# MLP up projection of a two-layer decoder trunk: high and low part of the input as one 512-column operand

## The chip, the cores and the metric

The kernel runs on one core of a Trainium2 chip. The metric is the device time of one execution in microseconds (us); lower is better. The time before is the median of three runs, 669.83 us (669.26 to 670.19). One further execution was profiled; its own time was 669.9 us.

## The reference: what is computed

The program is a decoder trunk with DEPTH = 2 layers over x of 256 tokens by 1024 features, float32. Each layer has a mixer (three kinds of attention heads that share one input and one output projection) and a gated MLP with a causal depthwise convolution of width 3; both are added to x. Cut to the MLP:

```python
def conv_glu_ffn(h, w_up, conv_w, conv_b, w_down):
    a, u = jnp.split(h @ w_up, 2, axis=-1)          # h: 256 x 1024, w_up: 1024 x 5632
    a = causal_depthwise_conv(a, conv_w) + conv_b    # width 3, per channel
    return (jax.nn.silu(a) * u) @ w_down             # w_down: 2816 x 1024

for i in range(DEPTH):
    x = x + hybrid_mixer(rmsnorm(x, norm1_g[i]), ...) @ w_out[i]
    x = x + conv_glu_ffn(rmsnorm(x, norm2_g[i]), w_up[i], conv_w[i], conv_b[i], w_down[i])
return rmsnorm(x, final_g)
```

## The kernel before

**Split operands.** Every large matrix product works on float32 numbers that are split in two: a high part, the value rounded to the fp32r format, and a low part, what the rounding left. A product is the sum of three: high by high, high by low, low by high. `weight` (L146 and behind) loads a weight tile by DMA into a staging buffer `st` (5 buffers, queue of SP), writes its high part into `hl` with a cast on ACT (L157) and its low part with a subtraction on DVE (L159). There are 8 buffers `hl`; a cast has to wait until an earlier tile's last matmul on PE has freed one. The activations are split in `transposed`: high by ACT (`ahi`, L195), low by DVE (`alo`, L196), with the tokens along the columns. Two functions hand out those tiles: `act_half` (four blocks of 128 features by 256 tokens, one tile for the high and one for the low parts) and `act_pair` (two halves, so all 1024 features).

**The MLP.** The 2816 channels are done in 11 groups f of 256 channels. `up(f)` loads four weight tiles of w_up (gate half `a` and value half `u`, each in two tiles of four feature blocks) and two tiles of w_down. For each of the two halves `au` and the two blocks of 128 channels `s` it runs over the eight blocks k of 128 features; each k takes three matmuls with 128 weight columns and 256 moving columns: high weights by `hhi` (L896), high weights by `hlo` (L897), low weights by `hhi` (L898). The sums stay in PSUM: one bank for `a` and one for `u`, each with s = 0 in the left 256 columns and s = 1 in the right. Roles u0 and u1 of two banks each take turns with f.

Behind the matmuls DVE multiplies `a` by the normalisation factors R (L900), ACT and DVE do the convolution (L906, L908), ACT a tanh (L911), DVE finishes the gate (L912), multiplies `u` by R/2 (L914) and by the gate (L915), and ACT and DVE split the product into `h_hi` (L919) and `h_lo` (L920).

`down(f)` multiplies h by the w_down rows of that group: 24 matmuls of 512 columns (L206 to L208, in `mm3`) into four banks `bn` that add up over all f. The loop runs `up(f)` and then `down(f - 1)`, so a group's elementwise work has a whole `up` to run beside. The last two groups' `down` comes at the end of the layer.

**What sets the order.** The tile framework orders each engine's instructions when the program is built and puts in the waits; at run time each engine takes its list in that order. DVE, ACT and PE each work in order, so an instruction that waits holds up all that stand behind it on its engine.

Of the kernel before, what the change touches and what calls it, by code (L numbers as in the profile page):

```python
# [12 lines left out]
F32 = mybir.dt.float32  # L13
FR = mybir.dt.float32r
BF = mybir.dt.bfloat16
AF = mybir.ActivationFunctionType
OP = mybir.AluOpType
AX = mybir.AxisListType

L = 256  # L20
# [50 lines left out]
def trunk(ctx, tc, x, norm1_g, w_in, cmp_pos, cmp_w1, cmp_w2, w_out, norm2_g, w_up, conv_w, conv_b, w_down,  # L71
          final_g, eye, consts_f, consts_b, out):
    nc = tc.nc
    V, S, G, PE = nc.vector, nc.scalar, nc.gpsimd, nc.tensor
# [3 lines left out]
    act = ctx.enter_context(tc.tile_pool(name="act", bufs=1))  # L78

    def banks(es, *layout):  # L80

        pools = {r: es.enter_context(tc.tile_pool(name="ps_" + r, bufs=n, space=bass.MemoryType.PSUM,
                                                  reuse_waits="tile")) for r, n in layout}
        return lambda r: pools[r].tile([128, 512], F32, name="b" + r, tag=r)
# [53 lines left out]
    def columns(b, dst, src):  # L138
        n = src.shape[0]
        PE.transpose(b[:, :n], src, ident[:n, :n])  # L140
        V.tensor_copy(dst, b[:, :n])


    def after(ins):
        return tc.issue_after(ins) if ins else nullcontext()
# [16 lines left out]
    def w_in_chunk(i, c0, n, then=None, behind=(None, None)):  # L162
        w = w_in[i].rearrange("(k p) c -> p k c", p=128)
        return [weight(w[:, 2 * h:2 * h + 2, c0:c0 + n], 2, n, then if h == 0 else None, behind)
                for h in range(4)]
# [15 lines left out]
    def new_ssq():  # L181
        return keep.tile([128, 2, 2], F32, name="ssq", tag="ssq", bufs=2)
# [14 lines left out]
        return l0, l1  # L197

    def act_half():
        return [act.tile([128, 4, L], FR, name=n, tag=n, bufs=3) for n in ("ahi", "alo")]  # L200

    def act_pair():
        return tuple(zip(act_half(), act_half()))
# [6 lines left out]
    for i in range(DEPTH):  # L210

        with ExitStack() as es:
            if i == 0:
                bank = banks(es, ("t", 2), ("d", 2), ("s", 2), ("o", 2))
            else:
                bank = banks(es, ("d", 2), ("s", 2), ("t", 2), ("o", 2))
# [5 lines left out]
            if i == 0:  # L222

                def idle(n):
                    b = bank("d")
                    for j in range(n):
                        PE.matmul(b[:, :256], zero[:, 0:128], zero, start=j == 0, stop=j == n - 1)

                idle(16)
                columns(bank("t"), cola[:, 0:16], rn)  # L230

                def other_half():
                    nc.scalar.dma_start(xr[:, 0, 512:D], x[0, 0:128, 512:D])
                    nc.sync.dma_start(xr[:, 1, 512:D], x[0, 128:256, 512:D])

                first = w_in_chunk(0, 0, 384, other_half)
                ssq = new_ssq()
                hhi, hlo = act_pair()
                for k0 in (0, 2, 4, 6):
                    last = transposed(bank, xr, gain1[i], hhi, hlo, k0, 2, role="tsso"[k0 // 2])  # L240
                idle(8)
                for t in range(2):
                    for n in range(2):
                        junk = pj.tile([128, 512], BF, name="junkv", tag="selb")
                        xs = xr[:, t, n * 512:(n + 1) * 512]
                        if n == 0:
                            with after(last[0].ins):
                                s0 = sumsq(ssq, t, n)
                            continue
                        with after(last[1].ins):  # L250
                            s1 = V.scalar_tensor_tensor(junk, xs, 1.0, xs, op0=OP.mult, op1=OP.mult,
                                                   accum_out=ssq[:, t, n:n + 1])
                squares = s0.ins, s1.ins
# [148 lines left out]
            def runs_of(segs):  # L402
# [5 lines left out]
                        r.append((t, [h], o, nk // 128))  # L408
                return r

            m0 = act_half()

            vv = pj.tile([128, 3, 2, 64], F32, name="vv")

# [349 lines left out]
            for _ in indexed(ob):  # L764
                fill(1)
            fill()
            m1 = act_half()
            ob = [o.rearrange("p c t q -> p c (t q)") for o in ob]
            split([z[64:128, 2:4, :] for z in m0], ob[0][64:128])
            split([z[0:64, 3, :] for z in m0], ob[0][0:64, 0])  # L770
# [77 lines left out]
            fill()  # L848
            dense.append(out_part((5, 6), (7,)))
            fill(3)  # L850
            hhi, hlo = act_pair()

            def half2(n):
                for t in range(2):
# [8 lines left out]
            R = keep.tile([128, 2, L], F32, name="R", tag="R", bufs=1)  # L863
            b = bank("t")
            for t in range(2):
                PE.matmul(b[:, t * 128:(t + 1) * 128], rstd[:, t:t + 1].to_broadcast([128, 128]), ident,
                          start=True, stop=True)
            S.copy(R[:, 0, :], b[:, :256])
            G.tensor_copy(R[:, 1, :], R[:, 0, :])
            R = R.rearrange("p a c -> p (a c)")  # L870


        with ExitStack() as es:
            order = ("n0", "n1", "u0", "u1") if i == 0 else ("n0", "u0", "n1", "u1")
            bank = banks(es, *((r, 2) for r in order))
            mp = es.enter_context(tc.tile_pool(name="mp", bufs=2, reuse_waits="tile"))
            dn = {}
            NF = DFF // 256
# [3 lines left out]
            def up(f):  # L882
                f0 = f * 256
                wh = [weight(wu[:, 4 * h:4 * h + 4, au * DFF + f0:au * DFF + f0 + 256], 4, 256)
                      for au in range(2) for h in range(2)]
                wd = [weight(w_down[i, (2 * f + s) * 128:(2 * f + s + 1) * 128, None, :], 1, 1024) for s in range(2)]
                bs = [bank(f"u{f % 2}") for _ in range(2)]
                order = [(au, s, range(8)) for au in range(2) for s in range(2)]
                if f == 0:
                    order = [(0, 0, range(4)), (1, 0, range(4)), (0, 0, range(4, 8)), (1, 0, range(4, 8)),  # L890
                             (0, 1, range(8)), (1, 1, range(8))]
                for au, s, ks in order:
                    o = bs[au][:, s * 256:(s + 1) * 256]
                    for k in ks:
                        wa, wl = (z[:, k % 4, s * 128:(s + 1) * 128] for z in wh[2 * au + k // 4])
                        PE.matmul(o, wa, hhi[k // 4][:, k % 4, :], start=k == 0, stop=False)  # L896
                        PE.matmul(o, wa, hlo[k // 4][:, k % 4, :], start=False, stop=False)  # L897
                        PE.matmul(o, wl, hhi[k // 4][:, k % 4, :], start=False, stop=k == 7)  # L898
                a = mp.tile([128, 512], F32, name="a", tag="a")
                V.tensor_tensor(a, bs[0], R, op=OP.mult)  # L900
                c = mp.tile([128, 512], F32, name="c", tag="c")
                for s in range(2):
                    cw = [colc[:, i, w * 22 + 2 * f + s:w * 22 + 2 * f + s + 1] for w in range(3)]
                    cw.append(cola[:, 32 + 22 * i + 2 * f + s:33 + 22 * i + 2 * f + s])
                    o = s * 256
                    S.activation(c[:, o:o + 256], a[:, o:o + 256], AF.Identity, bias=cw[3], scale=cw[2])  # L906
                    for w, d in ((1, 1), (0, 2)):
                        V.scalar_tensor_tensor(c[:, o + d:o + 256], a[:, o:o + 256 - d], cw[w], c[:, o + d:o + 256],  # L908
                                               op0=OP.mult, op1=OP.add)
                th = mp.tile([128, 512], F32, name="th", tag="th")  # L910
                S.activation(th, c, AF.Tanh, scale=0.5)  # L911
                V.scalar_tensor_tensor(th, th, 1.0, c, op0=OP.add, op1=OP.mult)  # L912
                u = mp.tile([128, 512], F32, name="u", tag="u")
                V.scalar_tensor_tensor(u, bs[1], 0.5, R, op0=OP.mult, op1=OP.mult)  # L914
                V.tensor_mul(u, u, th)  # L915
                h_hi = mp.tile([128, 2, L], FR, name="h_hi", tag="h_hi")
                h_lo = mp.tile([128, 2, L], FR, name="h_lo", tag="h_lo")
                u3 = u.rearrange("p (s c) -> p s c", s=2)
                S.copy(h_hi, u3)  # L919
                V.tensor_sub(h_lo, u3, h_hi.bitcast(F32))  # L920
                hs[f] = (h_hi, h_lo, wd)

            for n in range(2):
# [22 lines left out]
            fs = [NF - 2, NF - 1]  # L946
            ssq = new_ssq()
            if i < DEPTH - 1:
                hhi, hlo = act_pair()
                down(fs, [(0, 0), (0, 1)])  # L950
                add(0, 0)
                add(0, 1)
                down(fs, [(1, 0)])
                for t in range(2):
                    sumsq(ssq, t, 0)
                for k0 in (0, 2):
                    transposed(bank, xr, gain1[i + 1], hhi, hlo, k0, 2, role="u1")
                down(fs, [(1, 1)])
                add(1, 0)
                add(1, 1)  # L960
                for k0 in (4, 6):
                    transposed(bank, xr, gain1[i + 1], hhi, hlo, k0, 2, role="u1")
                for t in range(2):
                    sumsq(ssq, t, 1)
                continue
# [4 lines left out]
            for t in range(2):  # L970
                m0, m1, r = (keep.tile([128, 1], F32, name=f"fin{j}{t}") for j in range(3))
# [37 lines left out]
```

## Time and profile before

| | |
|---|---|
| median of three runs | 669.83 us (669.26 to 670.19) |
| profiled execution, its own time | 669.9 us |
| its span (first to last instruction) | 668.0 us |
| mean granted TensorE clock in the span | 0.992 |
| busy: PE, DVE, ACT, POOL | 645.2, 498.2, 374.3, 50.5 us |
| matmuls / of these in the up projection | 4403 / 2112 (704 each on L896, L897, L898) |
| MLP of layer 1, up(0) to the last matmul | 471.4 to 661.2 us of the span |

PE is the matmul engine and PEld its weight loads, which overlap the matmuls; DVE, ACT and POOL are the vector, scalar and GpSimd engines; SP issues most DMAs. A name such as `bu<-ahi,hl` means that a tile of kind bu (a bank of the up projection) is written from tiles ahi and hl. Matmuls are pipelined: a row's duration is longer than the distance to the next row's start, and that distance is what a matmul costs when PE has always more to do. This document calls it the step.

### The profile page before, as it was taken

Reading aid. Unit: us, or ns where it says so; the run is one execution under the profiler, and the core shown is the slowest. Engines: PE = TensorE matmul, PEld = TensorE weight load, DVE = VectorE, ACT = ScalarE, POOL = GpSimd, SP = SyncE. Lnnn points to the kernel's source line nnn. Section 1 sums busy time; section 2 is a strip of 40 time slices with the busy share of each in tenths; the row PEclk is TensorE's granted clock in tenths of the full one; section 3 lists DMA queues with packets and bytes.
Section 4 is the critical chain, followed back from the end, with each engine's and each line's share of the span. In section 5 each row is a group of like instructions: output and inputs, shape, how many; then the busy total and the mean of one; then the engine's idle time right before and its main releaser. Section 6 shows DMA issues by size and latency. Waiting matters only on the chain. (4 is left out here: it accounts for less than half of the span.)

```text
span 668.0 us, 11736 instructions
## 1 busy us (share of the span) xinstructions
PE 645.2 (97%) x4403; PEld 580.8 (87%) x4403; DVE 498.2 (75%) x1093; ACT 374.3 (56%) x683; POOL 50.5 (8%) x120
## 2 busy tenths in 40 slices
PE   6899999999999999999998999999999999999995
PEld 5887897779999999999988888877899999999994
DVE  3888999876877666666677799987596666666653
ACT  4656686756555555554374675786665544455522
POOL 3112210000000000000110132100000000000002
PEclk7999999999999999999999999999999999999998
DMA  7595134274666666665457525134466666666601
GB/s 246 167 300 163 42 118 127 66 241 132 198 188 187 189 189 190 186 187 170 134 150 226 148 80 171 51 117 150 144 196 188 186 189 189 189 190 188 189 1 63
DMA packets 76439, 107.34 MB, mean 161 GB/s; under 512 B 3717, under 2 KB 63286, under 8 KB 76384
## 3 DMA queue, kind: packets, MB, share of 16 engines
q1 hardware_dynamic: 75280, 104.35, 51.2%
q0 software_dynamic: 496, 1.21, 0.5%
q10 hardware_dynamic: 608, 1.06, 0.5%
q8 instruction: 34, 0.56, 0.3%
q14 instruction: 21, 0.17, 0.1%
HBM read 105.55 MB, written 1.05 MB: 160 GB/s over the span
## 5 line engine op out<-in xcount | busy, mean ns | idle before, releaser
L159 DVE TENSOR_TENSOR hl<-st,hl 128x1024 fp32r<-128x1024 f32 (+3 forms) x208 | 230.9, 1120 | 101.1 <-ACT hl L157 100.5
L157 ACT CAST hl<-st 128x1024 fp32r<-128x1024 f32 (+3 forms) x208 | 197.8, 970 | 143.2 <-PE bu L898 68.1
L897 PE MATMUL bu<-alo,hl 128*128 128x256 f32 x704 | 199.8, 284 | 0.8 <-DVE alo L196 0.8
L898 PE MATMUL bu<-ahi,hl 128*128 128x256 f32 x704 | 199.0, 283 | 0.0
L896 PE MATMUL bu<-ahi,hl 128*128 128x256 f32 x704 | 198.0, 283 | 0.0
L897 PEld LDWEIGHTS bu<-alo,hl 128*128 128x128 f32 x704 | 135.1, 192 | 1.9 <-DVE alo L196 1.2
L896 PEld LDWEIGHTS bu<-ahi,hl 128*128 128x128 f32 x704 | 134.5, 192 | 1.4 <-ACT ahi L195 0.5
L898 PEld LDWEIGHTS bu<-ahi,hl 128*128 128x128 f32 x704 | 135.1, 192 | 0.0
L206 PE MATMUL bd<-hl,ahi 128*128 128x384 f32 (+3 forms) x288 | 104.5, 366 | 1.7 <-ACT gate L525 1.0
L207 PE MATMUL bd<-hl,ahi 128*128 128x384 f32 (+3 forms) x288 | 101.9, 354 | 0.0
L208 PE MATMUL bd<-hl,alo 128*128 128x384 f32 (+3 forms) x288 | 101.2, 353 | 0.0
L206 PE MATMUL bn<-hl,h_hi 128*128 128x512 f32 x176 | 68.9, 392 | 0.0
L207 PE MATMUL bn<-hl,h_hi 128*128 128x512 f32 x176 | 68.6, 391 | 0.0
L208 PE MATMUL bn<-hl,h_lo 128*128 128x512 f32 x176 | 68.4, 390 | 0.0
L206 PEld LDWEIGHTS bd<-hl,ahi 128*128 128x128 f32 x288 | 54.6, 190 | 10.7 <-issue 2.2
L207 PEld LDWEIGHTS bd<-hl,ahi 128*128 128x128 f32 x288 | 54.7, 190 | 3.0 <-issue 1.0
L208 PEld LDWEIGHTS bd<-hl,alo 128*128 128x128 f32 x288 | 54.5, 189 | 2.9 <-issue 0.7
L208 PEld LDWEIGHTS bn<-hl,h_lo 128*128 128x128 f32 x176 | 33.1, 188 | 7.3 <-DVE h_lo L920 0.4
L206 PEld LDWEIGHTS bn<-hl,h_hi 128*128 128x128 f32 x176 | 33.1, 188 | 6.7 <-ACT h_hi L919 0.5
L207 PEld LDWEIGHTS bn<-hl,h_hi 128*128 128x128 f32 x176 | 33.1, 188 | 6.0
L908 DVE SCALAR_TENSOR_TENSOR c<-a,colc,c 128x255 f32<-128x255 f32 (+1 forms) x88 | 36.7, 477 | 0.7 <-ACT c L906 0.7
L911 ACT ACTIVATE th<-c 128x512 f32<-128x512 f32 x22 | 13.9, 632 | 35.1 <-DVE c L908 35.1
(235 smaller groups left out, 736.3 us busy)
## 6 DMA issues: line engine op xcount, KB each, us to landing
st<-in_w_up_dram SPq DMA_DIRECT2D x88, 512.0 KB, 3.7
st<-in_w_down_dram SPq DMA_DIRECT2D x44, 512.0 KB, 4.3
st<-in_w_in_dram SPq DMA_DIRECT2D x40, 384.0 KB, 3.8
st<-in_w_out_dram SPq DMA_DIRECT2D x12, 512.0 KB, 3.7
st<-in_w_in_dram SPq DMA_DIRECT2D x8, 360.0 KB, 3.6
st<-in_w_in_dram SPq DMA_DIRECT2D x8, 336.0 KB, 3.4
st<-in_w_out_dram SPq DMA_DIRECT2D x8, 256.0 KB, 3.1
xr<-in_x_dram ACTq DMA_DIRECT2D x2, 256.0 KB, 5.4
```

The lines of the kernel that those rows point to most:

```text
L157: S.copy(hv, sv)
L159: V.tensor_sub(lv, sv, hv.bitcast(F32))
L206: PE.matmul(b, ahi, whi, start=first, stop=False)
L207: PE.matmul(b, ahi, wlo, start=False, stop=False)
L208: PE.matmul(b, alo, whi, start=False, stop=last)
L896: PE.matmul(o, wa, hhi[k // 4][:, k % 4, :], start=k == 0, stop=False)
L897: PE.matmul(o, wa, hlo[k // 4][:, k % 4, :], start=False, stop=False)
L898: PE.matmul(o, wl, hhi[k // 4][:, k % 4, :], start=False, stop=k == 7)
L908: V.scalar_tensor_tensor(c[:, o + d:o + 256], a[:, o:o + 256 - d], cw[w], c[:, o + d:o + 256], op0=OP.mult, op1=OP.add)
L911: S.activation(th, c, AF.Tanh, scale=0.5)
```

## The change

The high and the low parts of the input now lie in one tile, `ahl`, side by side for each feature block, so that both form one operand of 512 columns. In `up(f)` each of the four passes (au, s) has a PSUM bank of its own. A pass first runs the eight products of the high weights with the 512-column operand (new L901): the left half of the bank gets high by high, the right half high by low. Then it adds the eight products of the low weights with `hhi`, 256 columns, to the left half (new L903). When a pass is complete, ACT copies the right half out of PSUM (`cross`, new L906) and DVE adds the left half to it (new L907) into `sa` or `su` in SBUF. The number of multiplied columns is the same: 512 + 256 for each k where it was 3 x 256.

The factor R/2 is now put on the gate (`th`) instead of on `u`. In the last group f = 10 the closing steps are done for each block s apart. The bank roles are now u0 for `a` and u1 for `u`. All other code is as before; the tile `ahl` replaces `ahi` and `alo` in the mixer too, where both halves are used as before.

```diff
     def act_half():
-        return [act.tile([128, 4, L], FR, name=n, tag=n, bufs=3) for n in ("ahi", "alo")]
+        z = act.tile([128, 4, 2, L], FR, name="ahl", tag="ahl", bufs=3)
+        return z[:, :, 0, :], z[:, :, 1, :], z
...
-            hhi, hlo = act_pair()
+            hhi, hlo, hhl = act_pair()
...
-                bs = [bank(f"u{f % 2}") for _ in range(2)]
                 order = [(au, s, range(8)) for au in range(2) for s in range(2)]
                 if f == 0:
                     order = [(0, 0, range(4)), (1, 0, range(4)), (0, 0, range(4, 8)), (1, 0, range(4, 8)),
                              (0, 1, range(8)), (1, 1, range(8))]
+                bs, sums = {}, [mp.tile([128, 2, L], F32, name=n, tag=n) for n in ("sa", "su")]
                 for au, s, ks in order:
-                    o = bs[au][:, s * 256:(s + 1) * 256]
-                    for k in ks:
-                        wa, wl = (z[:, k % 4, s * 128:(s + 1) * 128] for z in wh[2 * au + k // 4])
-                        PE.matmul(o, wa, hhi[k // 4][:, k % 4, :], start=k == 0, stop=False)
-                        PE.matmul(o, wa, hlo[k // 4][:, k % 4, :], start=False, stop=False)
-                        PE.matmul(o, wl, hhi[k // 4][:, k % 4, :], start=False, stop=k == 7)
-                a = mp.tile([128, 512], F32, name="a", tag="a")
-                V.tensor_tensor(a, bs[0], R, op=OP.mult)
+                    o = bs.get((au, s))
+                    if o is None:
+                        o = bs[au, s] = bank(f"u{au}")
+                    w = [[z[:, k % 4, s * 128:(s + 1) * 128] for z in wh[2 * au + k // 4]] for k in ks]
+                    for k, (wa, _) in zip(ks, w):
+                        PE.matmul(o, wa, hhl[k // 4][:, k % 4].rearrange("p z t -> p (z t)"), start=k == 0, stop=False)
+                    for k, (_, wl) in zip(ks, w):
+                        PE.matmul(o[:, :L], wl, hhi[k // 4][:, k % 4, :], start=False, stop=k == 7)
+                    if ks[-1] == 7:
+                        cross = mp.tile([128, L], F32, name="cross", tag="cross", bufs=4)
+                        S.copy(cross, o[:, L:])
+                        V.tensor_tensor(sums[au][:, s], o[:, :L], cross, op=OP.add)
+                        if s == 1 and au == 0:
+                            a = mp.tile([128, 512], F32, name="a", tag="a")
+                            V.tensor_mul(a, sums[0].rearrange("p s t -> p (s t)"), R)
...
                 V.scalar_tensor_tensor(th, th, 1.0, c, op0=OP.add, op1=OP.mult)
-                u = mp.tile([128, 512], F32, name="u", tag="u")
-                V.scalar_tensor_tensor(u, bs[1], 0.5, R, op0=OP.mult, op1=OP.mult)
-                V.tensor_mul(u, u, th)
+                V.scalar_tensor_tensor(th, th, 0.5, R, op0=OP.mult, op1=OP.mult)
+                u = mp.tile([128, 2, L], F32, name="u", tag="u")
...
-                S.copy(h_hi, u3)
-                V.tensor_sub(h_lo, u3, h_hi.bitcast(F32))
+                for z in (slice(0, 1), slice(1, 2)) if f == NF - 1 else (slice(0, 2),):
+                    V.tensor_mul(u[:, z], sums[1][:, z], th.rearrange("p (s t) -> p s t", s=2)[:, z])
+                    S.copy(h_hi[:, z], u[:, z])
+                    V.tensor_sub(h_lo[:, z], u[:, z], h_hi[:, z].bitcast(F32))
```

The built program shows where the instructions stand now. Line numbers behind the change are up to 11 higher.

**PE, one group f in the middle of layer 1.** Before, at the end of `down` (bn) and the start of the next `up` (bu), whose three rows then go round 32 times:

```order
L207 MATMUL bn_5473<-hl,h_hi 128x512
L208 MATMUL bn_5473<-hl,h_lo 128x512
L896 MATMUL bu_7190<-ahi,hl 128x256
L897 MATMUL bu_7190<-alo,hl 128x256
L898 MATMUL bu_7190<-ahi,hl 128x256
```

The same place with the change, a whole `up` in its four banks:

```order
L209 MATMUL bn_5288<-hl,h_hi 128x512
L210 MATMUL bn_5288<-hl,h_lo 128x512
L901 MATMUL bu_6537<-ahl,hl 128x512 x8
L903 MATMUL bu_6537<-ahl,hl 128x256 x8
L901 MATMUL bu_6557<-ahl,hl 128x512 x8
L903 MATMUL bu_6557<-ahl,hl 128x256 x8
L901 MATMUL bu_6579<-ahl,hl 128x512 x8
L903 MATMUL bu_6579<-ahl,hl 128x256 x8
L901 MATMUL bu_6599<-ahl,hl 128x512 x8
L903 MATMUL bu_6599<-ahl,hl 128x256 x8
```

The group has 64 matmuls where it had 96, and four changes from 256 to 512 columns (the last into `down`) where it had one.

**ACT, one group f in the middle of layer 1.** Before (hl are weight casts for this group's w_down and the next group's w_up):

```order
L157 CAST hl<-st 128x1024 x4
L906 ACTIVATE c<-a,cola,colc 128x256 x2
L911 ACTIVATE th<-c 128x512
L157 CAST hl<-st 128x1024 x2
L919 CAST h_hi<-u 128x512
```

With the change (the bu are the banks of the four passes, in the order of the PE rows above):

```order
L906 COPY cross<-bu_6537 128x256
L157 CAST hl<-st 128x1024
L906 COPY cross<-bu_6557 128x256
L157 CAST hl<-st 128x1024
L906 COPY cross<-bu_6579 128x256
L916 ACTIVATE c<-a,cola,colc 128x256 x2
L157 CAST hl<-st 128x1024
L906 COPY cross<-bu_6599 128x256
L157 CAST hl<-st 128x1024
L921 ACTIVATE th<-c 128x512
L157 CAST hl<-st 128x1024
L930 CAST h_hi<-u 128x512
```

Four copies stand between the casts, and the convolution's `c` now stands behind the copy of the third pass.

**PE at the start of the MLP, group f = 0 of layer 0.** Before (bt rows are transposes of the input's second half):

```order
L896 MATMUL bu_1890<-ahi,hl 128x256
L896 MATMUL bu_1891<-ahi,hl 128x256
L896 MATMUL bu_2037<-ahi,hl 128x256
L897 MATMUL bu_1890<-alo,hl 128x256
L898 MATMUL bu_1890<-ahi,hl 128x256
L897 MATMUL bu_1891<-alo,hl 128x256
```

With the change:

```order
L901 MATMUL bu_1886<-ahl,hl 128x512
L901 MATMUL bu_1895<-ahl,hl 128x512
L901 MATMUL bu_1926<-ahl,hl 128x512
L901 MATMUL bu_1948<-ahl,hl 128x512
L189 MATMUL bt<-ident,xr 128x128
L901 MATMUL bu_1886<-ahl,hl 128x512 x2
```

Three matmuls that needed the high part alone stood first; now the first matmul needs the low part too, and four of the first feature block stand ahead of the transposes.

More of the change, by code (lines that the diff above doesn't have):

```diff
@@ L409, in runs_of @@
                 return r
-            m0 = act_half()
+            m0 = act_half()[:2]
             vv = pj.tile([128, 3, 2, 64], F32, name="vv")
@@ L766, in trunk @@
             fill()
-            m1 = act_half()
+            m1 = act_half()[:2]
             ob = [o.rearrange("p c t q -> p c (t q)") for o in ob]
@@ L850, in trunk @@
             fill(3)
-            hhi, hlo = act_pair()
+            hhi, hlo, hhl = act_pair()
             def half2(n):
@@ L912, in up @@
                 V.scalar_tensor_tensor(th, th, 1.0, c, op0=OP.add, op1=OP.mult)
-                u = mp.tile([128, 512], F32, name="u", tag="u")
-                V.scalar_tensor_tensor(u, bs[1], 0.5, R, op0=OP.mult, op1=OP.mult)
-                V.tensor_mul(u, u, th)
+                V.scalar_tensor_tensor(th, th, 0.5, R, op0=OP.mult, op1=OP.mult)
+                u = mp.tile([128, 2, L], F32, name="u", tag="u")
                 h_hi = mp.tile([128, 2, L], FR, name="h_hi", tag="h_hi")
                 h_lo = mp.tile([128, 2, L], FR, name="h_lo", tag="h_lo")
-                u3 = u.rearrange("p (s c) -> p s c", s=2)
-                S.copy(h_hi, u3)
-                V.tensor_sub(h_lo, u3, h_hi.bitcast(F32))
+                for z in (slice(0, 1), slice(1, 2)) if f == NF - 1 else (slice(0, 2),):
+                    V.tensor_mul(u[:, z], sums[1][:, z], th.rearrange("p (s t) -> p s t", s=2)[:, z])
+                    S.copy(h_hi[:, z], u[:, z])
+                    V.tensor_sub(h_lo[:, z], u[:, z], h_hi[:, z].bitcast(F32))
                 hs[f] = (h_hi, h_lo, wd)
@@ L948, in trunk @@
             if i < DEPTH - 1:
-                hhi, hlo = act_pair()
+                hhi, hlo, hhl = act_pair()
                 down(fs, [(0, 0), (0, 1)])
```

## The prediction

> **What bounds the kernel now.** I read the busy times first, then PE's two MLP stretches, then the order of time inside one group f. The busy times and the stretches (158 to 330 us is layer 0's MLP, 478 to 650 us layer 1's):
>
> ```profile
> PE 645.2 (97%) x4403; PEld 580.8 (87%) x4403; DVE 498.2 (75%) x1093; ACT 374.3 (56%) x683; POOL 50.5 (8%) x120
> 158.00:330.00 172.00, 172.00 (x1232) 162.96 (x1231) 122.37 (x160) 86.49 (x105) 2.52 (x8) 1.00 0.59 179
> 478.00:650.00 172.00, 172.00 (x1243) 163.38 (x1242) 118.15 (x155) 83.54 (x102) 1.05 (x2) 1.00 0.55 168
> ```
>
> The columns are PE, PEld, DVE, ACT, POOL, granted clock, DMA share, GB/s. In both stretches PE is never idle and runs at full clock, while DVE is busy for 0.69 to 0.71 of the time and ACT for half. So there only a cheaper stream of matmuls saves time, and what DVE and ACT get on top is free until they make PE wait. What a matmul costs is the step, the distance between starts. One group, from its first `up` row through `down` to the next `up`:
>
> ```profile
> 536.55 0.28 PE L896 MATMUL bu<-ahi,hl 128*128 128x256 f32 x1
> ...
> 548.06 0.40 PE L206 MATMUL bn<-hl,h_hi 128*128 128x512 f32 x1
> 548.30 0.40 PE L207 MATMUL bn<-hl,h_hi 128*128 128x512 f32 x1
> ...
> 549.45 0.39 PE L206 MATMUL bn<-hl,h_hi 128*128 128x512 f32 x1
> ...
> 553.30 0.39 PE L208 MATMUL bn<-hl,h_lo 128*128 128x512 f32 x1
> 553.53 0.28 PE L896 MATMUL bu<-ahi,hl 128*128 128x256 f32 x1
> 553.64 0.28 PE L897 MATMUL bu<-alo,hl 128*128 128x256 f32 x1
> ```
>
> The 96 matmuls of 256 columns take 548.06 - 536.55 = 11.51 us, a step of 0.1199. The 24 of 512 columns take 5.47 us. The last 17 steps of these (549.45 to 553.30) are 0.2265 each; the first six (548.06 to 549.45) take 1.39 us where six such steps would be 1.36, so the change of width costs about 0.03. The step back to 256 columns is 0.11, 0.01 short. Twice the columns thus cost 0.2265 instead of 0.2398: each matmul has some 0.013 us that don't depend on its width. The group's period is 553.53 - 536.55 = 16.98 us.
>
> **The change part by part.** *PE in a steady group.* For each of 32 pairs (k, pass) two matmuls of 256 columns become one of 512; the third stays. A pass is then eight wide steps with a change of width, 1.39 + 2 x 0.2265 = 1.84, and eight narrow ones, 0.96 less the 0.01 of the first: 2.79. Four passes: 11.17, against 11.51. That saves 0.34; since the first narrow step behind `down` was short before too, I take 0.32 a group, or 22 x 0.32 = 7.0 us over both layers. Without a cost at the changes of width it would be 32 x (0.2398 - 0.2265) = 0.426 a group, 9.4 us: the upper end. If all wide steps were as slow as the first six (1.39 / 6 = 0.2317), 32 x 0.0081 = 0.26 a group or 5.7 us: the lower end. I take the first sum, because the same slow start shows behind another group's `up`, in the last fence of this part (649.94 to 651.33, again 1.39 us).
>
> The Trainium skill (TensorE: Matmul & The Clock Gate, "Back-to-back issue gap") gives N / 2.4 ns plus a floor of 2.5 ns a matmul. By that, 704 matmuls fewer are worth 1.8 us, and the sum would be near no change. The rows disagree: 0.1199 where the rule has 0.109. The measured steps go into the sum.
>
> *DVE and ACT in a steady group.* Added are four copies of 128x256 from PSUM on ACT and four sums of 128x256 with one PSUM operand on DVE. The nearest rows:
>
> ```profile
> L353 ACT CAST ksw<-bt 128x256 fp32r<-128x256 f32 x4 | 1.5, 373 | 3.4 <-DVE u L532 3.4
> L195 ACT ACTIVATE ahi<-bt,cola 128x256 fp32r<-128x256 f32 x18 | 7.7, 471 | 0.5 <-DVE alo L196 0.4
> L354 DVE TENSOR_TENSOR ksw<-bt,ksw 128x256 fp32r<-128x256 f32 x4 | 1.7, 424 | 0.6 <-ACT ksw L353 0.5
> L914 DVE SCALAR_TENSOR_TENSOR u<-bu,R 128x512 f32<-128x512 f32 x22 | 15.2, 690 | 3.2 <-PE bu L898 1.0
> L915 DVE TENSOR_TENSOR u<-u,th 128x512 f32<-128x512 f32 x22 | 15.1, 685 | 0.1
> 536.55:553.53 16.98, 16.98 (x121) 16.02 (x120) 11.75 (x15) 8.36 (x11) 0.00 (x0) 1.00 0.62 187
> ```
>
> A copy is 0.37 to 0.47, a sum about 0.42 and surely under 0.69 (a row of twice the width). R/2 on the gate instead of on `u`, and `a` from SBUF instead of PSUM, change nothing: 0.690 and 0.685 for the two sources. So DVE goes from 11.75 to about 13.5 and ACT from 8.36 to about 10.1 us of a 16.66 us group. These 1.7 us each cost nothing while PE covers them; without the cover they would be 22 x 1.7 = 37 us. The margin of the cover:
>
> ```profile
> 558.04 1.05 ACT L157 CAST hl<-st 128x1024 fp32r<-128x1024 f32 x1 [2.99 <-PE bu L898]
> 560.98 1.09 ACT L906 ACTIVATE c<-a,cola,colc 128x256 f32<-128x256 f32 x2 [0.45 <-DVE a L900]
> 567.70 0.62 ACT L919 CAST h_hi<-u 128x512 fp32r<-128x512 f32 x1 [1.40 <-DVE u L915]
> 568.72 0.69 DVE L920 TENSOR_TENSOR h_lo<-u,h_hi 128x512 fp32r<-128x512 f32 x1
> ```
>
> This group's `up` began at 553.53, its `h_lo` is done at 569.41, and its `down` begins at 553.53 + 16.98 + 11.51 = 582.0: 12.6 us to spare. With the change ACT's copies wait for PE: behind the third pass's copy stand the convolution's `c` and two casts. That copy can start 8.4 us into the group, so `c` starts near 9.9 where it was 560.98 - 553.53 = 7.45. The chain behind it (c, tanh, gate, product, split) then has four more instructions of 0.4 between its parts, and I get `h_lo` near 19 us into the group, against a need at 16.66 + 11.17 = 27.8. About 8 us stay. The casts for the next group's first weights still wait for the second pass (4.5 us into the group at 558.04, now about 5.2) and are needed at 16.7. A bank is emptied a microsecond or two behind its pass and next written 14 us later. DMAs are issued when DVE's subtraction frees a staging buffer:
>
> ```profile
> SPq L153 <- DVE hl L159: 99.6, 39, 4.5
> st<-in_w_up_dram SPq DMA_DIRECT2D x88, 512.0 KB, 3.7
> ```
>
> The buffer freed is used again five tiles later, some 14 us, and the transfer takes 3.7 once issued; a subtraction that is 3 us late still leaves cover. I cost all of this at nothing.
>
> *Start of each MLP.* The first matmul now needs `alo` too:
>
> ```profile
> 471.37 0.52 PE L896 MATMUL bu<-ahi,hl 128*128 128x256 f32 x3
> 472.52 0.38 PE L897 MATMUL bu<-alo,hl 128*128 128x256 f32 x1 [0.62 <-DVE alo L196]
> 471.98 0.87 DVE L196 SCALAR_TENSOR_TENSOR alo<-bt,cola,ahi 128x256 fp32r<-128x256 f32 x2
> 473.37 0.86 DVE L196 SCALAR_TENSOR_TENSOR alo<-bt,cola,ahi 128x256 fp32r<-128x256 f32 x2
> ```
>
> Three matmuls, 0.36 us, ran before that wait and now come behind it; the four wide ones that are ready then last until 473.3, and the next blocks' `alo` ends from 473.8 to 474.2, so PE idles there a little longer too. I take 0.45 us for each layer, 0.9 in all; the ends are nothing (the transposes and the second half of `alo` decide anyway) and 1.5 each.
>
> *End of each MLP.* The last `up` and what hangs on it:
>
> ```profile
> 649.82 0.28 PE L898 MATMUL bu<-ahi,hl 128*128 128x256 f32 x1
> 649.94 0.40 PE L206 MATMUL bn<-hl,h_hi 128*128 128x512 f32 x1
> ...
> 651.33 0.39 PE L206 MATMUL bn<-hl,h_hi 128*128 128x512 f32 x1
> ...
> 652.01 0.76 PE L206 MATMUL bn<-hl,h_hi 128*128 128x512 f32 x2
> 652.60 0.40 PE L207 MATMUL bn<-hl,h_hi 128*128 128x512 f32 x1
> 650.14 0.69 DVE L914 SCALAR_TENSOR_TENSOR u<-bu,R 128x512 f32<-128x512 f32 x1 [1.03 <-PE bu L898]
> 651.60 0.62 ACT L919 CAST h_hi<-u 128x512 fp32r<-128x512 f32 x1 [3.21 <-DVE u L915]
> ```
>
> Two steps from 652.01 take 0.59 instead of 0.45: `h_hi`, done at 652.22, is 0.14 late. With the change the first block's `h_hi` comes after a copy (0.37), a sum, a product (0.42 each), a cast (0.37) and 0.04 between each: 650.14 + 1.70 = 651.84, in time. I take a gain of 0.1 for each layer.
>
> *Sum:* -7.0 + 0.9 - 0.2 = -6.3 us. The profiled execution, 668.0 of span and 669.9 in all, becomes 661.7 and 663.6; its own time lies 0.07 above the median, so I predict **663.5 us**.
>
> **The rivals.** *Nothing for the change of width, and no loss at the starts:* -9.4 - 0.2, 660.2 us. For it: the late steps are 0.2265 to the end; against: both places show the slow start. *The starts cost more:* 1.5 us each, 669.8 - 7.0 + 3.0 - 0.2 = 665.6. For it: the row with 0.62 of idle time stands there already; against: the work ahead of the transposes is only put off. *The fixed 0.013 us belongs to the pair, not to the matmul:* if a wide step of this operand were 0.2373, just 0.0025 under two narrow ones, 704 x 0.0025 = 1.8 is saved and 0.7 lost: 668.7, no change that can be told. Every 512-column row speaks against it. (That is the result that the Trainium skill's floor of 2.5 ns gives.) *Slower: DVE becomes the bound.* If the sums, which read PSUM while PE writes its neighbour banks, cost 1.38 each (twice the 0.69 of the wide row), DVE needs 11.75 + 5.5 = 17.3 us a group; PE then waits for `h_lo`, and 20 groups at +0.3 and 0.7 at the ends make 676.5. It decides from (16.98 - 11.75) / 4 = 1.31 us a sum. Against it: L914 reads PSUM at 0.690 in that very loop.
>
> **How the numbers follow.** Forecast 0.72; no cost of width 0.10; dear starts 0.07; pair rival 0.05; DVE 0.06. The forecast's own range is 661.3 to 665.0 (the ends of the step, 5.7 to 9.4, with the starts). To hold 8 in 10, and since a dear start can meet the lower end of the step, I give 660.4 to 667.0; it leaves out the last two rivals and half of the first. A change of 0.2% (1.3 us) is about what can be told here: faster 0.87, within 0.06, slower 0.07.
>
> **What would show it.** Steps of L901 of 0.227 to 0.232 and of L903 of 0.120; a group period near 16.66; no wait of PE between the MLP's start and its end; DVE near 13.5 us a group. The forecast falls if PE shows waits on `cross` or the sums inside the loop, if L901 takes 0.237 or more, or if the idle time at either start passes 2 us.

## The result and the profile after

The changed kernel takes 663.18 us (661.65 to 664.11) beside 670.01 us of the kernel before in the same series (669.26 to 670.6): a ratio of 0.9891, 95% interval 0.9864 to 0.9918. A second series of five rounds gave 662.0 against 669.79, ratio 0.9885 (0.9868 to 0.9902). Forecast were 663.5, range 660.4 to 667.0, and "faster". One execution at a granted clock of 0.85 for its whole length took 705.83 us; it is left out, and the profile shown below is one of the second series (its span 658.4 us).

The busy times, and the two stretches of the MLP that the prediction opened with (the same columns: PE, PEld, DVE, ACT, POOL, granted clock, DMA share, GB/s):

```profile
PE 636.7 (97%) x3699; PEld 542.2 (82%) x3699; DVE 532.5 (81%) x1185; ACT 399.4 (61%) x773; POOL 49.8 (8%) x120
158.00:330.00 172.00, 172.00 (x910) 147.93 (x908) 141.97 (x208) 99.56 (x153) 2.42 (x9) 1.00 0.62 184
478.00:650.00 172.00, 171.93 (x910) 147.89 (x909) 139.27 (x207) 96.61 (x149) 2.84 (x5) 1.00 0.55 166
```

PE still has no idle time there worth the name (0.07 us in 344). DVE rose from 0.71 and 0.69 of the stretch to 0.83 and 0.81, ACT from 0.50 and 0.49 to 0.58 and 0.56: still covered. So PE's stream decides, as before, and it is read by the distances between starts. One steady group of layer 1, PE's order of time, with its four passes and the first and last rows of `down`:

```profile
529.36 1.98 PE L901 MATMUL bu<-ahl,hl 128*128 128x512 f32 x8
531.17 1.11 PE L903 MATMUL bu<-ahl,hl 128*128 128x256 f32 x8
532.12 2.00 PE L901 MATMUL bu<-ahl,hl 128*128 128x512 f32 x8
533.96 1.12 PE L903 MATMUL bu<-ahl,hl 128*128 128x256 f32 x8
534.92 2.00 PE L901 MATMUL bu<-ahl,hl 128*128 128x512 f32 x8
536.76 1.12 PE L903 MATMUL bu<-ahl,hl 128*128 128x256 f32 x8
537.71 2.00 PE L901 MATMUL bu<-ahl,hl 128*128 128x512 f32 x8
539.55 1.11 PE L903 MATMUL bu<-ahl,hl 128*128 128x256 f32 x8
540.50 0.40 PE L208 MATMUL bn<-hl,h_hi 128*128 128x512 f32 x1
...
545.74 0.39 PE L210 MATMUL bn<-hl,h_lo 128*128 128x512 f32 x1
545.97 0.61 PE L901 MATMUL bu<-ahl,hl 128*128 128x512 f32 x2
```

The group's period is 545.97 - 529.36 = 16.61 us, and all its neighbours have it (529.36, 545.97, 562.58, 579.20, ...); it was 16.98. `down` takes 5.47 as before; `up` takes 11.14 instead of 11.51. Three passes have eight wide matmuls in 1.84 us. The first pass has them in 1.81, eight steps of 0.2265: it stands behind `down`, whose matmuls are 512 columns wide too, so no change of width lies ahead of it. The narrow eight take 0.95 or 0.96.

What each layer's MLP takes, from the last matmul of the mixer's output projection (`bd`) to the last of `down` (`bn`), worked out from the starts of those matmuls in the two profiles:

| us | layer 0 before | after | layer 1 before | after | both |
|---|---|---|---|---|---|
| start: last `bd` to first `bn` | 25.65 | 25.33 | 25.98 | 25.68 | -0.62 |
| end: last `up` matmul to last `bn` | 11.79 | 12.02 | 11.01 | 11.19 | +0.41 |
| whole MLP | 190.14 | 186.76 | 189.70 | 186.27 | -6.81 |
| mixer of layer 1 | | | 131.96 | 132.03 | +0.07 |

The MLPs explain -6.81 us. The two spans differ by 9.6 us (668.0 and 658.4), but the rest lies before layer 0's MLP, where neither kernel's order of matmuls differs and where the first loads land: up to the last `bd` of layer 0 the profiles of all the kernels below scatter from 146.2 to 149.6 (PE's wait for the input x alone is 4.3 us in the profile before, 3.0 in e1, 1.0 here and none in e11). So a single span is no measure of this change; the MLP stretch is, to about 0.1 us (a second profile of the changed kernel has 186.72 and 186.27).

The start of layer 1's MLP:

```profile
464.98 0.39 PE L210 MATMUL bd<-hl,ahl 128*128 128x512 f32 x1
466.36 1.21 PE L901 MATMUL bu<-ahl,hl 128*128 128x512 f32 x4 [0.99 <-DVE ahl L196]
467.83 0.30 PE L189 MATMUL bt<-ident,xr 128*128 128x128 f32 x1 [0.26 <-DVE ahl L196]
```

The same place before, with the rows that the prediction did not show:

```profile
471.14 0.39 PE L208 MATMUL bd<-hl,alo 128*128 128x512 f32 x1
473.57 0.28 PE L896 MATMUL bu<-ahi,hl 128*128 128x256 f32 x1
473.99 0.30 PE L189 MATMUL bt<-ident,xr 128*128 128x128 f32 x1
```

PE now stands idle for 0.99 where it had 0.62. Since the mixer's last matmul (465.0) 1.4 us have gone by when the first `up` matmul starts; before, the low part let PE go on at 472.52, 1.4 us after that last matmul (471.14) too, but three matmuls had been done by then. In front of the transposes PE is idle for 0.26, where it was 0.14 before (L896 ends at 473.85). Both ups that lie in the start stretch should have saved 2 x 0.367 = 0.73 and the stretch got shorter by 0.32 and 0.30, so each start lost 0.42.

The end of layer 1's MLP, DVE's and ACT's rows and PE's around its first wait:

```profile
639.90 0.69 DVE L922 SCALAR_TENSOR_TENSOR th<-th,c 128x512 f32<-128x512 f32 x1 [0.76 <-ACT th L921]
640.18 0.40 PE L208 MATMUL bn<-hl,h_hi 128*128 128x512 f32 x1
640.38 0.37 ACT L906 COPY cross<-bu 128x256 f32<-128x256 f32 x1 [0.51 <-PE bu L903]
640.63 0.69 DVE L923 SCALAR_TENSOR_TENSOR th<-th,R 128x512 f32<-128x512 f32 x1
641.24 0.42 DVE L907 TENSOR_TENSOR su<-bu,cross 128x256 f32<-128x256 f32 x1
641.57 0.75 DVE L929 TENSOR_TENSOR u<-su,th 128x256 f32<-128x256 f32 x2
642.02 0.39 PE L210 MATMUL bn<-hl,h_lo 128*128 128x512 f32 x1
642.02 0.74 ACT L930 CAST h_hi<-u 128x256 fp32r<-128x256 f32 x2 [1.27 <-DVE u L929]
642.48 0.19 PEld L208 LDWEIGHTS bn<-hl,h_hi 128*128 128x128 f32 x1 [0.49 <-ACT h_hi L930]
642.82 0.40 PE L209 MATMUL bn<-hl,h_hi 128*128 128x512 f32 x1
```

ACT's copy is done at 640.75, but DVE adds the two halves only from 641.24: its next instruction is L923, R/2 on the gate, from 640.63 to 641.32. The first `h_hi` is done near 642.4, and the weight load that needs it (it is `h_hi` that PE takes as weights here) goes at 642.48. PE's step there is 642.48 - 642.02 = 0.46 instead of 0.23, and the next one, to 642.82, is 0.11 too long. I read that as the price of the weight load, which starts together with its matmul here (both at 642.48) and about 0.23 us, a whole step, ahead of it in the rows before; no run varied it.

### The profile page after: what moved, and what is told of

Its sections match the earlier page's. It is cut to its first block, busy times and chain, and to the rows that moved or that the text cites. A ratio compares the mean times of both kernels' runs of the same rounds, so it can differ in the third digit from the quotient of the medians.

```text
span 704.1 us, 10527 instructions
## 1 busy us (share of the span) xinstructions
PE 686.6 (98%) x3699; PEld 568.1 (81%) x3699; DVE 537.3 (76%) x1185; ACT 400.1 (57%) x773; POOL 51.1 (7%) x120
## 3 DMA queue, kind: packets, MB, share of 16 engines
q10 hardware_dynamic: 608, 1.06, 0.4%
## 5 line engine op out<-in xcount | busy, mean ns | idle before, releaser
L901 PE MATMUL bu<-ahl,hl 128*128 128x512 f32 x704 | 193.1, 418 | 1.1 <-DVE ahl L196 1.1
L901 PEld LDWEIGHTS bu<-ahl,hl 128*128 128x128 f32 x704 | 130.2, 193 | 33.9 <-DVE ahl L196 2.0
L208 PE MATMUL bd<-hl,ahl 128*128 128x384 f32 (+3 forms) x288 | 109.8, 384 | 1.8 <-ACT gate L527 0.7
L903 PEld LDWEIGHTS bu<-ahl,hl 128*128 128x128 f32 x704 | 101.2, 194 | 10.8
L209 PE MATMUL bd<-hl,ahl 128*128 128x384 f32 (+3 forms) x288 | 107.0, 372 | 0.0
L210 PE MATMUL bd<-hl,ahl 128*128 128x384 f32 (+3 forms) x288 | 106.7, 372 | 0.0
L903 PE MATMUL bu<-ahl,hl 128*128 128x256 f32 x704 | 104.1, 292 | 0.0
L209 PE MATMUL bn<-hl,h_hi 128*128 128x512 f32 x176 | 73.6, 418 | 0.0
L208 PE MATMUL bn<-hl,h_hi 128*128 128x512 f32 x176 | 73.5, 417 | 0.0
L210 PE MATMUL bn<-hl,h_lo 128*128 128x512 f32 x176 | 73.1, 416 | 0.0
L208 PEld LDWEIGHTS bd<-hl,ahl 128*128 128x128 f32 x288 | 55.8, 194 | 12.7 <-issue 2.6
L906 ACT COPY cross<-bu 128x256 f32<-128x256 f32 x88 | 32.5, 369 | 52.9 <-PE bu L903 52.9
L209 PEld LDWEIGHTS bd<-hl,ahl 128*128 128x128 f32 x288 | 56.2, 195 | 4.2 <-issue 1.1
L210 PEld LDWEIGHTS bd<-hl,ahl 128*128 128x128 f32 x288 | 55.7, 194 | 4.2 <-issue 0.8
L916 ACT ACTIVATE c<-a,cola,colc 128x256 f32<-128x256 f32 x44 | 24.1, 595 | 9.6 <-DVE a L910 9.6
L907 DVE TENSOR_TENSOR sa<-bu,cross 128x256 f32<-128x256 f32 x44 | 18.5, 421 | 9.6 <-ACT cross L906 7.5
```

The source lines that it names most:

```text
L208: PE.matmul(b, ahi, whi, start=first, stop=False)
L209: PE.matmul(b, ahi, wlo, start=False, stop=False)
L210: PE.matmul(b, alo, whi, start=False, stop=last)
L901: PE.matmul(o, wa, hhl[k // 4][:, k % 4].rearrange("p z t -> p (z t)"), start=k == 0, stop=False)
L903: PE.matmul(o[:, :L], wl, hhi[k // 4][:, k % 4, :], start=False, stop=k == 7)
L906: S.copy(cross, o[:, L:])
```

## The experiments

Each ran on the chip beside the kernel before, whose medians were 669.79 (e0 to e3), 669.96 (e4 to e8) and 670.62 (e9 to e11). The theory: in the loop PE's stream alone decides, and it got shorter by the cost that each matmul has whatever its width; ACT's copies and DVE's sums are covered; each start loses by the wait for the low part. The rivals were those of the prediction.

### e0: the changed kernel again

> The changed kernel once more, for a profile at full clock. Theory (each matmul has about 0.013 us that do not depend on its width, and a change from 256 to 512 columns costs about 0.03): 662 to 664 us; a pass of eight L901 takes 1.84 us, eight L903 0.95, a group 16.66. Rival (no cost of width): a pass of eight L901 takes 1.81, a group 16.56, and the time is 661 or less.

662.0 us, ratio 0.9885 (0.9868 to 0.9902). It is the measure for what follows, and the profile above.

### e1: the wide operand taken away, all else left

```diff
-PE.matmul(o, wa, hhl[k // 4][:, k % 4].rearrange("p z t -> p (z t)"), start=k == 0, stop=False)
+PE.matmul(o[:, :L], wa, hhi[k // 4][:, k % 4, :], start=k == 0, stop=False)
+PE.matmul(o[:, L:], wa, hlo[k // 4][:, k % 4, :], start=False, stop=False)
```

> Each wide matmul of the changed kernel is split into two of 256 columns, one for each half of the same bank; copies, sums, banks and all else stay. Theory (the gain is the number of matmuls): the group goes back to 17.0 us, 22 x 0.34 = 7.4 us slower than the changed kernel, less up to 1 us since the first matmuls of the MLP need the high part alone again: 668.5 to 670. Rival (the gain comes from the new banks, the earlier sums or the closing steps): as fast as the changed kernel, 662 to 663.

670.51 us, ratio 1.0007 (0.9995 to 1.0019): the whole gain is gone, and copies, sums, banks and order are all as in the changed kernel. One group of it, order of time of PE and busy times of the group (columns as above):

```profile
520.19 0.28 PE L901 MATMUL bu<-ahl,hl 128*128 128x256 f32 x1
520.31 0.28 PE L902 MATMUL bu<-ahl,hl 128*128 128x256 f32 x1
520.43 0.28 PE L901 MATMUL bu<-ahl,hl 128*128 128x256 f32 x1
520.19:537.17 16.98, 16.98 (x121) 16.02 (x120) 13.57 (x20) 9.47 (x15) 0.00 (x0) 1.00 0.61 188
```

Steps of 0.12 and a period of 16.98, exactly that of the kernel before. DVE has 13.57 us a group where it had 11.75, and that costs nothing. The starts of e1 are those of the kernel before (25.64 and 25.98), the ends those of e0 (12.01 and 11.23): the loss at the starts comes with the wide operand, the loss at the ends with the new closing steps. So the gain is that of the 704 fewer matmuls, and the rest of the change costs 0.4 us at the ends, less than the interval can tell. The "pair" rival has fallen: split in two, a wide matmul takes 0.240 where it has 1.84 / 8 = 0.230.

With it falls what the Trainium skill's rule (TensorE: Matmul & The Clock Gate, "Back-to-back issue gap": N / 2.4 ns and 2.5 ns more, there called the gap of an isolated matmul) would have given, 1.8 us for 704 matmuls: e1 has just these more than e0 and takes 8.5 us longer, 12 ns each.

A third width bears out that the fixed cost is no oddity of the 256-column steps. In the mixer of the kernel before, matmuls of 384 columns between neighbours of their own width follow each other at 0.174 us (median of 360 steps), where a straight line from 0.120 at 256 to 0.2265 at 512 gives 0.173. The line ends somewhere below 256: 128-column matmuls, mostly transposes, follow each other at 0.108 and not at 0.067. One thing the runs don't separate: every matmul here has a weight load of its own (PEld counts as many as PE, 4403 before and 3699 now), so each matmul that went took its load with it, and how the 0.013 us divide between the two stays open.

### e2: a change of width at every matmul

```diff
-for k, (wa, _) in zip(ks, w):
+for k, (wa, wl) in zip(ks, w):
     PE.matmul(o, wa, hhl[k // 4][:, k % 4].rearrange("p z t -> p (z t)"), start=k == 0, stop=False)
-for k, (_, wl) in zip(ks, w):
     PE.matmul(o[:, :L], wl, hhi[k // 4][:, k % 4, :], start=False, stop=k == 7)
```

> In each pass wide and narrow matmuls alternate for each k, where the changed kernel has eight wide ones and then eight narrow ones: 32 changes from 256 to 512 columns in a group instead of 4. Theory (a change of width costs 0.03, less 0.01 on the way back): 28 x 0.02 = 0.56 us a group, 12 us slower than the changed kernel, 674. Rival (the slow first steps behind a change of width are a filling that is paid once in a long stretch, not at each change): 662 to 663, as the changed kernel.

663.99 us, ratio 0.9917 (0.9903 to 0.993). One `up` of it:

```profile
515.62 0.40 PE L901 MATMUL bu<-ahl,hl 128*128 128x512 f32 x1
515.85 0.28 PE L902 MATMUL bu<-ahl,hl 128*128 128x256 f32 x1
515.97 0.40 PE L901 MATMUL bu<-ahl,hl 128*128 128x512 f32 x1
516.21 0.28 PE L902 MATMUL bu<-ahl,hl 128*128 128x256 f32 x1
515.28:532.07 16.79, 16.79 (x89) 14.31 (x88) 13.72 (x20) 9.68 (x15) 0.00 (x0) 1.00 0.61 191
```

A wide step is 0.236 on the mean and a narrow one 0.117: the wide one loses 0.010 against 0.2265, the narrow one wins back 0.003. The period is 16.79, so 28 more changes to the wide operand cost 16.793 - 16.613 = 0.18 us, 0.0065 each with the way back. Over 22 groups that is 4.0 us; the starts give 2.0 of it back (they are 24.71 and 25.06, 0.62 shorter than e0's although both ups in them are 0.18 slower), and 663.99 - 662.0 = 2.0 is left. The sign of my expectation was right (the change of width costs something) and its price a change was three times too large: I had carried most of what the first six steps behind a long narrow run lose (0.03 in all) over to a single step. The gain at the starts I had not seen at all; e9 takes it up.

### e3 and e4: the cover of DVE and ACT, used up on purpose

In e3 each pass is copied and summed a second time, in e4 four times, into tiles that nobody reads (e3's edit; e4 has `range(3)`):

```diff
 V.tensor_tensor(sums[au][:, s], o[:, :L], cross, op=OP.add)
+for _ in range(1):
+    crossx = mp.tile([128, L], F32, name="crossx", tag="crossx", bufs=2)
+    S.copy(crossx, o[:, L:])
+    more = mp.tile([128, L], F32, name="more", tag="more", bufs=2)
+    V.tensor_tensor(more, o[:, :L], crossx, op=OP.add)
```

> Each pass is copied and summed a second time into tiles that nobody reads: four more copies on ACT and four more sums on DVE in a group. Theory (PE covers them, DVE comes to about 15.3 us of a 16.66 us group): no change against the changed kernel, within 0.2%. Rival (the copies and sums already stand on the path, through ACT's order): 1.7 us a group or a part of it, up to 37 us slower.

> Each pass is copied and summed four times (three times into tiles that nobody reads): 16 copies and 16 sums in a group. Theory (the sums are free only while DVE stays below PE's group of 16.61 us): DVE needs 11.75 + 16 x 0.42 = 18.5 us, becomes the bound, and about 20 groups at +1.9 make some 38 us: 700 (690 to 706), with PE waiting for banks or for h_lo. Rival (PE hides them by buffers however long they are): 662.

e3 takes 662.51 us, ratio 0.989 (0.9874 to 0.9905), which can't be told from e0. Its groups keep the period of 16.61; here the busy times of one, and those of one of e0:

```profile
516.54:533.15 16.61, 16.61 (x89) 14.33 (x88) 14.80 (x24) 10.51 (x19) 0.00 (x0) 1.00 0.64 208
```

```profile
529.36:545.97 16.61, 16.61 (x89) 14.34 (x88) 13.34 (x20) 9.43 (x15) 0.00 (x0) 1.00 0.62 190
```

DVE and ACT do 1.46 and 1.08 us more a group between those borders (four sums and four copies, some across the border), and PE sees none of it; only the end of layer 0 is longer, 12.58 us where e0 has 12.02. So in the loop copies and sums at their single price cost nothing either. e4 takes 709.11 us, ratio 1.058 (1.0531 to 1.0628). The two MLP stretches and PE's longest waits in it:

```profile
150.00:355.00 205.00, 187.70 (x967) 156.86 (x966) 189.53 (x351) 142.78 (x298) 3.49 (x12) 0.98 0.51 157
503.00:700.00 197.00, 181.22 (x925) 151.30 (x923) 181.29 (x339) 135.36 (x283) 4.41 (x6) 0.99 0.46 145
...
PE bn L208 <- ACT h_hi L935: 17.5, 6, 7.2
PE bu L903 <- DVE hl L159: 7.1, 10, 1.2
PE bu L901 <- DVE more L912: 5.1, 9, 1.6
```

Here the rival's mechanism is seen: twelve more sums of 0.419 are 5.03 us a group, 13.34 + 5.03 = 18.4 is over the 16.61 that PE needs, and PE waits for `h_hi`, for the low parts of the weights and for its banks. DVE, busy for 0.92 of the time, is the bound. So DVE as the bound is a real case, and the change stays 3.3 us away from it in the group shown. The price came out 9 us over my 700 and outside my 690 to 706: DVE's need alone gives 20 groups x 1.8 = 35 us over e0, and 47 were measured. The MLP stretches, 210.92 and 205.45, hold 43.3 of these: 25.2 between the start and the end, 1.4 for each of 18 groups and so less than DVE's need, 3.6 at the starts, and 14.5 at the ends (21.12 and 16.58). The size is no clean price of DVE's load: the extra tiles have two buffers each, so that ACT waits for DVE's sums (27.5 us) and DVE for ACT's copies (22.0 us), and the built program cuts `up` and `down` into shorter turns on PE than e0's.

### e5: the first feature blocks as two narrow matmuls

```diff
 for k, (wa, _) in zip(ks, w):
+    if f == 0 and s == 0 and k < 2:
+        PE.matmul(o[:, :L], wa, hhi[k // 4][:, k % 4, :], start=k == 0, stop=False)
+        PE.matmul(o[:, L:], wa, hlo[k // 4][:, k % 4, :], start=False, stop=False)
+        continue
```

> In the first group of each MLP the wide matmuls of the first two feature blocks of the first two passes are split into two of 256 columns, so that PE can begin with the high part alone. Theory (PE loses 0.4 us at each start, since its first matmul waits for the low part): from the last matmul of the output projection to the first matmul of group 2 takes 0.3 us less in each layer, 661.4 us in all. Rival (the transposes of the second half decide the start): no change in that stretch.

661.61 us, ratio 0.9875 (0.9848 to 0.9902), not to be told from e0 by the time. The profile can: the start stretches are 25.09 and 25.42 where e0 has 25.33 and 25.68, and PE's wait is shorter (here PE's waits for the split input, of e0 and of e5: us in total, times, longest):

```profile
PE bu L901 <- DVE ahl L196: 1.5, 2, 1.0
```

```profile
PE bu L903 <- DVE ahl L196: 1.1, 2, 0.7
```

So the wait for the low part is a good half of the loss at the start: letting the high part begin returns 0.25 of its 0.42 us, although four more matmuls a layer have to be paid.

### e7: R/2 on the convolution's result, beside the tanh

```diff
-V.scalar_tensor_tensor(th, th, 1.0, c, op0=OP.add, op1=OP.mult)
-V.scalar_tensor_tensor(th, th, 0.5, R, op0=OP.mult, op1=OP.mult)
+cr = mp.tile([128, 512], F32, name="cr", tag="cr")
+V.scalar_tensor_tensor(cr, c, 0.5, R, op0=OP.mult, op1=OP.mult)
+V.scalar_tensor_tensor(th, th, 1.0, cr, op0=OP.add, op1=OP.mult)
```

> The factor R/2 is put on the convolution's result c, beside the tanh, and the gate is (tanh + 1) times that: one DVE instruction less behind the tanh, as many in all. Theory (at the end of each MLP the multiplication by R/2 stands on DVE ahead of the last sum and makes the first h_hi 0.23 us late): the stretch from the last up matmul to the last down matmul is 0.2 us shorter in each layer, 661.6 us in all. Rival (the copy of the last pass decides): that stretch stays at 11.2 and 12.0.

661.94 us, ratio 0.9876 (0.9851 to 0.9902); the time can't tell it from e0. The ends are 11.90 and 10.99 us, where e0 has 12.02 and 11.19 and the kernel before 11.79 and 11.01. The rows of layer 1's end:

```profile
640.70 0.69 DVE L923 SCALAR_TENSOR_TENSOR cr<-c,R 128x512 f32<-128x512 f32 x1
640.75 0.64 ACT L921 ACTIVATE th<-c 128x512 f32<-128x512 f32 x1 [1.28 <-DVE c L918]
641.50 0.69 DVE L924 SCALAR_TENSOR_TENSOR th<-th,cr 128x512 f32<-128x512 f32 x1
641.70 0.40 PE L208 MATMUL bn<-hl,h_hi 128*128 128x512 f32 x1
642.57 0.42 DVE L907 TENSOR_TENSOR su<-bu,cross 128x256 f32<-128x256 f32 x1
```

The product with R now runs beside the tanh, and the last sum starts 642.57 - 641.70 = 0.87 us behind the first `down` matmul instead of 641.24 - 640.18 = 1.06, although a product of the first block now stands ahead of it. So L923 in its place between the gate and the last sum cost layer 1's end all of its loss (0.18) and layer 0's half of it (0.12 of 0.23); what the other half is was not taken apart.

### e8: e5 and e7 together

> The narrow start and the early R/2 together. Theory: both losses are got back, 661 us, 0.8 to 1.0 us below the changed kernel. Rival: no difference that can be measured.

661.48 us, ratio 0.9863 (0.9832 to 0.9894). The MLP stretches are 186.39 and 185.87 us, 0.37 and 0.40 under e0's, close to the 0.27 + 0.12 and 0.26 + 0.20 of the two alone.

### e9 and e10: wide and narrow in turn in the first group, e11: the changed kernel beside them

e9 is e7, and in group 0 alone each wide matmul is followed by its narrow one, so that low weights by `hhi` fill the start. e10 is e9 with the first block's wide matmul as two narrow ones, the high part first. The new lines of e9, without those of e7:

```diff
+wide = [(o, wa, hhl[k // 4][:, k % 4].rearrange("p z t -> p (z t)"), k == 0, False)
+        for k, (wa, _) in zip(ks, w)]
+low = [(o[:, :L], wl, hhi[k // 4][:, k % 4, :], False, k == 7) for k, (_, wl) in zip(ks, w)]
+for z, wt, x, first, last in chain(*zip(wide, low)) if f == 0 else wide + low:
+    PE.matmul(z, wt, x, start=first, stop=last)
```

> The early R/2, and in the first group of each MLP wide and narrow matmuls alternate for each k; all later groups keep eight wide and eight narrow. Theory (with the narrow matmuls of the first feature block, which need only what is already there, PE has work while it waits for the next blocks): from the last output projection matmul to the first down matmul 24.7 to 24.9 us in layer 1, where the changed kernel has 25.68, and 0.2 less at the ends: 660 us. Rival (the stretch was shorter in the kernel that alternates everywhere because both of its groups alternate): 25.6, 661.8 us.

> As the one before, and the wide matmul of the first feature block is split into two narrow ones, so that the high part alone can begin. Theory: PE starts 0.7 us earlier and then waits for the next blocks; 0.2 to 0.4 us less than the one before in that stretch, 24.4, 659.6 us. Rival (what follows waits for the transposes anyway): the same 24.8.

> The changed kernel beside these two on the same chip: 662 us, first down matmul 25.7 us behind the output projection in layer 1.

661.19 us (ratio 0.9861, 0.9844 to 0.9877) for e9, 661.21 (0.9864, 0.9848 to 0.988) for e10, 661.91 (0.9871, 0.9857 to 0.9886) for e11. The intervals overlap, so the times don't separate the three; e9 has the lowest median of all the kernels run. The MLP stretches do: e9 has 186.10 and 185.63, e11 186.72 and 186.27, 0.62 and 0.64 more. In e9's start stretch, 24.80 and 25.19, the second wait is gone, as the rows of its layer 1 show (e0's are above):

```profile
467.88 1.68 PE L904 MATMUL bu<-ahl,hl 128*128 128x512 f32 x8 [0.99 <-DVE ahl L196]
469.41 0.27 PE L189 MATMUL bt<-ident,xr 128*128 128x128 f32 x1
```

Eight matmuls now run from the first feature block where four did, and the transposes find their data ready. e10 shortens neither stretch further (24.79 and 25.18). Its waits say why:

```profile
PE bt L189 <- DVE ahl L196: 1.2, 2, 0.7
```

PE starts at once, and then waits 0.73 in front of the transposes: the wait for the split input is put off, not shortened. What stays is the wait for the split on DVE; a faster split was not tried. e2, in which all groups alternate, has starts of 24.71 and 25.06 although its second group is 0.18 slower; so about 0.3 more is to be had behind group 0 as well, and what brings it wasn't settled.

## Why the prediction was right

The forecast's mechanism holds, and the two other views of the loop agree with it: without the wide operand the gain is nil (e1), with the sums doubled it stays (e3). Point by point against the sum of -6.3 us, which the profiles give as -6.81:

| term | predicted | measured | by |
|---|---|---|---|
| loop, 22 groups | -7.0 (0.32 each) | -8.07 (0.367 each) | period 16.98 to 16.613 |
| two starts | +0.9 | +0.85 | start stretches |
| two ends | -0.2 | +0.41 | end stretches |

**The loop** was mis-sized by about 1 us, within its bounds of 5.7 to 9.4. The step was "A pass is then eight wide steps with a change of width", taken four times: the pass itself is right (2.79 predicted; 1.84 + 0.95 measured), but the first pass stands behind `down`, which is as wide, so a group has three changes and not four. That is 0.03 a group. The other 0.02 I gave away when I took 0.32 for a worked-out 0.34: the short narrow step that I named for it was in the 11.51 already. Together 0.047 x 22 = 1.0 us.

**The starts** were right, both in what is lost (three matmuls, 0.36, and a little idle time behind) and in its cause: the wait at the first matmul went from 0.62 to 0.99, e1 has none of the loss, and e5 and e9 took back part of it.

**The ends** are the step that failed. I wrote: "With the change the first block's `h_hi` comes after a copy (0.37), a sum, a product (0.42 each), a cast (0.37) and 0.04 between each". The four prices hold (0.37, 0.42, 0.37 to 0.42, 0.4). What I left out is that the product with R/2, moved from `u` to the gate, is done by the same DVE and is still running when the copy is done: 0.5 us between copy and sum. In the kernel before, that product stood in the chain too, as L914; I took it out and put nothing in its place. e7 shows it: with L923 beside the tanh, the ends are 0.12 and 0.20 shorter, 11.90 and 10.99; layer 0's is still 0.11 longer than before, and I don't know why. And the gain I hoped for was small anyway: 0.11 of the 0.14 I took for lateness of `h_hi` is the step behind the first matmul with the fresh `h_hi`, and it is there in e7 too, where that matmul itself waits 0.06. The two errors, -1.07 and +0.61, are opposite in sign, and that is luck: it is why the total came within half a microsecond.

**The cover** held. DVE took 13.34 us in the group shown (13.5 predicted), a copy 0.37, a sum 0.42, and `h_lo` was done 19.0 us into that group (about 19 predicted):

```profile
L906 ACT COPY cross<-bu 128x256 f32<-128x256 f32 x88 | 32.5, 370 | 39.9 <-PE bu L903 39.7
L907 DVE TENSOR_TENSOR su<-bu,cross 128x256 f32<-128x256 f32 x44 | 18.4, 417 | 2.0 <-ACT cross L906 2.0
```

The sum has the price of the attention's sum of the same shape (0.424), not that of the rival (1.38). PE has no wait inside the loop; its only new ones are those at the starts and ends.

**The rivals.** No cost of width with no loss at the starts: fell, since the slow first steps are there (1.84 against 1.81) and the starts lost 0.85; but at three changes a group it is nearer than I had it. Dear starts: fell, the idle time is 1.25 and not over 2. The pair: fell by e1. DVE as the bound: fell here; e4 shows that it exists, from a load that four times the sums reach and twice do not. The 1.31 us a sum from which I let it decide is where the gain is used up; PE would begin to wait from (16.61 - 11.75) / 4 = 1.2.

**What is left open.** The measured gains of 6.8, 7.8 and 8.7 us (three series) lie at or above the 6.8 that the MLP stretches explain. The part before the first MLP scatters by more than that from profile to profile, so I can't say whether the excess belongs to the change; e1, which shares everything but the wide operand, shows none (+0.5 us with an interval from -0.3 to +1.3).

## What to carry to other kernels

Where PE is the bound and matmuls share their weights, put their moving operands side by side: here each matmul that went away with its weight load was worth 11.5 ns net (0.367 us for 32), and in the loop engines with a fifth of their time free carried the extra copies and sums for nothing. Count changes of width between neighbours over the whole loop, its seam included. And when a factor is moved from one operand to another, follow it on the engine that applies it: off the loop's critical path it is free, but at the layer's end it stood right in front of the sum that PE was waiting for.

## What the hardware showed that I had not expected

Changing the width at every matmul costs next to nothing: 0.0065 us for a change to 512 columns and back (e2). Behind a run of narrow matmuls the first five wide steps lose 0.03 together; where each run is one matmul long, a wide step loses 0.010 and the narrow one behind it wins back 0.003 (0.117, where it is 0.120 in a run of its own). And at the end of layer 1 the step behind the first matmul with the fresh `h_hi` was 0.11 us too long in each of six profiles (before, e0, e1, e7, e8, e11), whether that first matmul was 0.03 late (before) or 0.29 (e1). I read it as a weight load in the open, since the weights were only just produced; the runs show the 0.11, not its cause.
